# Summing a modulation half-vector on TensorE: as columns with the weight block stationary, instead of as a row and on VectorE

## The chip, the cores and the metric

The program runs on one core of one Trainium2 chip. The metric is device time in microseconds (us) of one execution. The median of three runs of the kernel before is 2114.07 us (2113.8 to 2114.29). The execution that was profiled took 2113.91 us; its span from the first to the last instruction is 2112.2 us.

## The reference

One layer of a streaming encoder on x of 1024 tokens by 1024 features, in float32: a SwiGLU block, a mixer of two attention branches, and a second SwiGLU block. Each of the three sub-layers is modulated by vectors that come from the conditioning vector c:

```python
cond = jax.nn.silu(c)
mod = (cond @ ada_w[l] + ada_b[l]).reshape(B, N_SUBLAYERS, 3, D_MODEL)
h = modulate(x, norm_g[l, 0], mod[:, 0, 0], mod[:, 0, 1])      # shift, scale
x = x + 0.5 * mod[:, 0, 2][:, None, :] * swiglu(h, ffn1_w1[l], ffn1_w3[l], ffn1_w2[l])
```

`modulate` is `rms_norm(x, g) * (1 + scale) + shift`. `ada_w` has 1024 rows and 9 x 1024 columns: column group 0 gives the first shift, group 1 the first scale. The first product of the layer needs h, and so the first shift, the first scale and the root mean square of each token of x.

## The kernel before, in words

x lies transposed: tile `x[i][j]` has 128 features as partitions and 512 of the tokens (half j). The big products are made in float32 from three fast passes each (`mm3`: high part times high, high times low, low times high, where a value is split into a rounded part made by ScalarE and the rest made by VectorE). Such a pass is one MATMUL of 128x512; the tiles `wh`, `wl` are the parts of a weight, and `h` is a part of the modulated x.

All instructions between two calls of `flush` are recorded first and then put in order by a planner (`Plan`). It has a table of prices for each operation (`length`, L359), counts due times back from TensorE's work (`deadlines`), and lets each engine, SyncE's DMA queue among them, take the task that can start first, by due time (`place`). Numbers in `FOUND` (L197) fix, for each flush, the planner's settings and a list of seeds; each seed shifts the due times of a random run of tasks by some us (`moved`). For a flush that `FOUND` does not name, the planner tries the settings in `PLANS` and keeps the best by its own reckoning. There are six flushes: 1 is the opening with the whole first SwiGLU block, 2 the end of that block, 3 and 4 the projections and the index scores, 5 the two attentions, 6 the output products and the second SwiGLU block. An order once chosen is fixed in the program: each engine works its list off in that order and waits where an input is missing.

The opening loads the first token half of x (eight tiles of 256 KB) and the blocks `mraw` of `ada_w`: for a half-vector of 512 columns, eight blocks (kc = 0 to 7) of 128 rows by 512 columns. The class `ModHalf` (L1584) turns the eight blocks into four columns of 128 values in a TensorE bank `b`, and `mod_done` (L1672) adds `ada_b` to them (VectorE, tile `mod`); for the scale it also makes `A`. Two half-vectors are needed for the first product, and before the change they take different ways:

- the scale, `mod[1, 0]`: VectorE multiplies each block by its column of the condition and adds it up in `macc` (`add`, eight instructions); then `columns` (L1609) sums `macc` over its partitions by four matmuls, with a 128x128 block of `macc` stationary and the column `ones_col` moving.
- the shift, `mod[0, 0]`: `row` (L1623) makes eight matmuls with a column of the condition stationary (128x1) and the block moving (512 columns), which gives the sum as a row; ScalarE copies it (`mrow`); `columns_of_row` (L1616) turns it into columns by four matmuls.

These matmuls are plain float32. The list counts one call for each of them; the trace shows two records for each call (four calls on `nacc` are eight records), each with its own LDWEIGHTS, the load of the stationary operand.

Beside that, squares of x (ScalarE, `nsq`) are added on VectorE (`nacc`), summed by four matmuls (`norm_rms`, L676), made into `nr` by twelve small VectorE instructions (`norm_root`), and spread over the partitions by four matmuls with `ident` moving (`norm_spread`, L694). Then `block` (L1716) makes, for four feature tiles, `x <- x * A * spread` (VectorE, `scale`) and the two parts of h (`pair`: ScalarE adds the shift `mod` and rounds, VectorE makes the rest). The weights `wr` of the first products are loaded behind the `mraw` blocks. Four matmuls on zeros (`zr`) that set up banks stand at the very start. The second token half and the modulation half-vectors `mod[1, 1]`, `mod[0, 1]` follow while products run.

Of the kernel before, what the change touches and what calls it, by code (L numbers as in the profile page):

```python
# [16 lines left out]
AF = mybir.ActivationFunctionType  # L17
# [45 lines left out]
class View:  # L63


    def __init__(self, tile, ops):
        self.tile, self.ops = tile, ops
# [117 lines left out]
def real(v):  # L185
# [9 lines left out]
         (10, 0.15, 0, 2, 300, 15, 3), (30, 0.02, 0, 6, 400, 1e9, 2), (30, 0.0, 0, 4, 600, 20, 1), (10, 0.15, 2, 4, 400, 20, 3)]  # L195
VERBOSE = False
FOUND = {  # L197
# [5 lines left out]
}  # L203


# [35 lines left out]
class Plan:  # L241
# [6 lines left out]
    def __init__(self, tc):  # L248
        self.tc, self.on, self.tasks, self.behind = tc, False, [], 0
        self.free = {e: 0.0 for e in self.ENGINES}  # L250
        self.wire, self.done, self.flushes = 0.0, {}, 0
        self.kept, self.wanted, self.spans = {}, [], []
        self.port = {"vector": 0.0, "gpsimd": 0.0}
        for e in self.ENGINES:
            setattr(self, e, PlanEngine(self, e))
# [88 lines left out]
    def close(self):  # L344

        self.on = False
        for x in self.kept.values():
            if x.slot is not None:
                self.slots(x).append((x.end, x.slot))
        self.kept = {}  # L350
# [8 lines left out]
    def length(self, t, e):  # L359

        n = t.n
        if t.dma:
            return 0.06 if e == "sync" else ISSUE, 0.0
        if e == "tensor":
            if t.took:
                return t.took, 0.23
            if t.turn:
                d = TURN[0]
            elif t.exact:
                d = max(0.04, 0.0133 + n / 2400.0) + (0.004 if t.dear and n == 512 else 0.0)  # L370
            elif t.op == "transpose":
                d = n / 1174.0
            else:
                d = max(0.224, 0.009 + n / 595.0)
            return d, 0.23
        more = "accum_out" in t.kw
        if e == "scalar":
            ap = sum(isinstance(t.kw.get(x), View) for x in ("bias", "scale"))
            return (0.055 if t.near else 0.1) + n / 1200.0 + (0.12 if more else 0.0) + (0.06 if ap else 0.0) + (0.13 if t.calls[0][1][0].tile.kw.get("name") == "yt" else 0.0), 0.14
        if e == "gpsimd":  # L380
            if t.op in ("tensor_scalar", "memset"):
                return 0.24 + n / 1230.0, 0.105
            return 0.06 + n / 440.0, 0.105
        if t.op == "tensor_tensor_scan":
            d = 0.15 + n / 480.0
        elif t.op == "tensor_tensor_reduce":
            d = 0.08 + n / 960.0
        elif t.op == "scalar_tensor_tensor" or more:
            d = 0.13 + n / 960.0
        elif t.op == "tensor_scalar" and t.port:  # L390
            d = 0.065 + n / 1920.0
        else:
            d = 0.068 + n / 960.0
        return max(0.09 if t.op == "reciprocal" else 0.075, d), 0.16
# [281 lines left out]
def norm_rms(k, acc, tmp, ptile):  # L676

    nc = k.nc
    ps = ptile()
    for b in range(4):  # L680
        nc.tensor.matmul(ps[:, b:b + 1], acc[:, b * 128:b * 128 + 128], k.ones_col, start=True, stop=True)
    return norm_root(k, ps[:, 0:4], tmp)


def norm_root(k, t, tmp):

    v = tmp.tile([128, 4], F32, tag="nv", name="nv", bufs=1)
    k.nc.vector.tensor_scalar(v, t, 1.0 / D, EPS, op0=ALU.mult, op1=ALU.add)
    r = tmp.tile([128, 4], F32, tag="nr", name="nr", bufs=1)
    rsqrt(k, r, v, tmp, "na", 1)  # L690
    return r
# [892 lines left out]
class ModHalf:  # L1584
# [28 lines left out]
            self.k.nc.tensor.matmul(t[:, b:b + 1], self.acc[:, b * 128:b * 128 + 128], self.k.ones_col, start=True, stop=True)  # L1613
        mod_done(self.k, self.i, t, 4 * self.h, 4)

    def columns_of_row(self, row):  # L1616

        t = self.bank()
        for b in range(4):
            self.k.nc.tensor.matmul(t[:, b:b + 1], row[0:1, b * 128:b * 128 + 128], self.k.ones_col[0:1, :], start=True, stop=True)  # L1620
        mod_done(self.k, self.i, t, 4 * self.h, 4)

    def row(self):  # L1623

        k, nc = self.k, self.k.nc
        t = self.bank()
        for kc in range(8):
            nc.tensor.matmul(t[0:1, :], k.cond[:, kc:kc + 1], self.raws[kc], start=kc == 0, stop=kc == 7)
        r = self.tile("mrow")
        nc.scalar.activation(r[0:1, :], t[0:1, :], AF.Copy)  # L1630
        return r

    def steps(self, d_row):

# [37 lines left out]
def mod_done(k, i, t, b0, n):  # L1672
    nc = k.nc
    m = k.mod[:, i * 8 + b0:i * 8 + b0 + n]
    nc.vector.tensor_add(m, t[:, 0:n], k.ada_b[:, i * 8 + b0:i * 8 + b0 + n])
    s, j = i // 3, i % 3
    c8 = slice(s * 8 + b0, s * 8 + b0 + n)
    if j == 1:
        nc.vector.scalar_tensor_tensor(k.A[:, c8], m, 1.0, k.ng[:, c8], op0=ALU.add, op1=ALU.mult)
    elif j == 2:  # L1680
        nc.vector.tensor_scalar(k.G[:, c8], m, 0.5, None, op0=ALU.mult)
# [540 lines left out]
def layer(tc, xT, c, pos, ada_w, ada_b, ng, inv, w13a, w2a, w_a, w_f, w_q, w_g, fb, fg, dg, wbr, wout, w13b, w2b, out):  # L2222
    with ExitStack() as es:
        k = K()
# [59 lines left out]
        with ExitStack() as ph:  # L2284
# [21 lines left out]
            mod = {(i, h): ModHalf(k, i, h, bank) for h in range(2) for i in range(2)}  # L2306
# [61 lines left out]
                mod[0, 0].load(n + 1)  # L2368
            for i in range(4):
                pairs[i].load1("c", (0,))  # L2370
            rms[0] = norm_rms(k, sq.acc, rp, bank)
            mod[1, 0].add(8)
            ops.rb[0] = norm_spread(k, rms[0], bank)
            row = mod[0, 0].row()
            mod[1, 0].columns()
            mod[0, 0].columns_of_row(row)
            for c in range(4):
                ops.block(c)
            for i in range(4):
# [314 lines left out]
```

## Time and profile before

| | |
|---|---|
| median of three runs | 2114.07 us (2113.8 to 2114.29) |
| the profiled execution | 2113.91 us, span 2112.2 us |
| TensorE busy | 2090.3 us, 99% of the span |
| VectorE busy | 1593.7 us, 75% |
| ScalarE busy | 1126.3 us, 53% |
| GpSimd busy | 356.6 us, 17% |
| first product (`b<-h,wh`) starts | 26.79 us |
| attentions (flush 5) | about 999 to 1295.6 us |

In a row of the timeline stand the start, the length, the engine, the line, the operation, the tile written and the tiles read, the shape and the count of instructions merged into the row; in square brackets the idle time of the engine just before and what ended it. PE is TensorE's matmul, PEld its weight load, DVE VectorE, ACT ScalarE, POOL GpSimd, SPq the issue of DMAs by SyncE. Almost all instructions carry L261, the planner's one issuing line, so they are told apart by their tiles. In a table by stretches of time stand the length of the stretch, the busy time and count of records for each engine, the TensorE clock granted (1.00 is full), the DMA share and the DMA rate.

### The profile page before, as it was taken

What the parts mean: (1) busy time and instruction counts of PE and PEld (TensorE: products, weight loads), DVE (VectorE), ACT (ScalarE), POOL (GpSimd) and SP (SyncE); (2) the same over time, 40 slices, a digit from 0 to 9 for tenths busy, and PEclk for the clock granted to TensorE, in tenths of its full rate; (3) what the DMA queues carried; (4) which work ended last, traced back from release to release, by engine and by line L of the source; (5) the groups of instructions that cost most, each with busy time, mean ns of one, the idle gap of its engine ahead of it and who ended that gap; (6) DMA issues with size and microseconds to landing.
All of it is one profiled execution on the core that took longest, in us unless ns stands there. A gap on an engine that the chain in (4) does not pass through costs nothing.

```text
span 2112.2 us, 31881 instructions
## 1 busy us (share of the span) xinstructions
PE 2090.3 (99%) x10548; PEld 1747.4 (83%) x10548; DVE 1593.7 (75%) x3118; ACT 1126.3 (53%) x2088; POOL 356.6 (17%) x595
## 2 busy tenths in 40 slices
PE   7999999999999999999999999999999999999999
PEld 5888888878888999998888777878888888888887
DVE  7988887869977388775799887697975765558754
ACT  5645444446556285876887775234633333334443
POOL 0013332312101100001545441001011011000000
PEclk9999999999999999999999999999999999999999
DMA  9358887899842325457876766595143434166611
GB/s 356 110 160 292 277 285 258 275 393 387 283 137 98 99 91 196 178 185 255 296 264 232 251 234 245 172 333 192 45 135 124 161 102 138 65 241 253 224 63 43
DMA packets 207959, 429.21 MB, mean 203 GB/s; under 512 B 33192, under 2 KB 51624, under 8 KB 207792
## 3 DMA queue, kind: packets, MB, share of 16 engines
q1 hardware_dynamic: 175392, 321.49, 45.0%
q0 software_dynamic: 32400, 105.67, 13.2%
q8 instruction: 83, 1.36, 0.3%
q14 instruction: 84, 0.69, 0.1%
HBM read 279.48 MB, written 109.83 MB: 184 GB/s over the span
## 4 chain that ended last, share of the span: by engine, by line
PE 92%; DMA 4%; DVE 3%; ACT 1%; issue 1%; SPq 0%; DVEq 0%; ACTq 0%
PE b L261 39%; PE y L261 27%; PE pj L261 13%; PE py L261 7%; PE p L261 4%; PE pt L261 3%; DMA a<-in_w2a 1%; DMA mraw<-in_ada_w 1%; DVE wl L261 0%; DVE h L261 0%; DMA nat<-d_qkv 0%; DMA wr<-in_w13a 0%; DMA wr<-in_wout 0%; DMA pre<-in_w_g 0%; DVE z L261 0%
## 5 line engine op out<-in xcount | busy, mean ns | idle before, releaser
L261 PE MATMUL b<-h,wh 128*128 128x512 f32 x1552 | 483.0, 391 | 2.7 <-ACT h L261 2.6
L261 ACT ACTIVATE wh<-wr 128x512 fp32r<-128x512 f32 x312 | 195.5, 630 | 368.6 <-PE b L261 157.4
L261 PE MATMUL y<-h,wh 128*128 128x512 f32 x1168 | 361.0, 389 | 0.0
L261 PEld LDWEIGHTS b<-h,wh 128*128 128x128 f32 x1552 | 292.1, 189 | 65.4 <-ACT h L261 2.7
L261 DVE TENSOR_TENSOR wl<-wr,wh 128x512 fp32r<-128x512 f32 x312 | 213.0, 687 | 148.6 <-ACT wh L261 148.3
L261 PE MATMUL b<-h,wl 128*128 128x512 f32 x776 | 303.1, 391 | 0.0
L261 PEld LDWEIGHTS y<-h,wh 128*128 128x128 f32 x1168 | 219.1, 188 | 46.1 <-ACT y L261 0.3
L261 PE MATMUL y<-h,wl 128*128 128x512 f32 x584 | 227.2, 389 | 0.0
L261 PE MATMUL pj<-wh,h 128*128 128x384 f32 (+1 forms) x768 | 175.5, 319 | 0.0
L261 PEld LDWEIGHTS b<-h,wl 128*128 128x128 f32 x776 | 146.2, 188 | 30.7
L261 POOL DMA_DIRECT2D d_g<-z x154 | 83.6, 544 | 502.0 <-DVE z L261 485.9
L261 DVE TENSOR_TENSOR wl<-a,wh 128x512 fp32r<-128x512 f32 x132 | 90.6, 687 | 63.6 <-ACT wh L261 61.6
L261 ACT ACTIVATE wh<-g 128x512 fp32r<-128x512 f32 x154 | 96.0, 624 | 78.2 <-PE b L261 49.1
L261 PE MATMUL b<-wl,wh 128*128 128x512 f32 x352 | 136.7, 389 | 0.6 <-DVE wl L261 0.6
L261 ACT ACTIVATE wh<-a 128x512 fp32r<-128x512 f32 x132 | 82.4, 624 | 102.2 <-PE b L261 55.5
L261 PE MATMUL b<-wh 128*128 128x512 f32 x352 | 136.8, 389 | 0.0
L261 PE MATMUL b<-wh,wl 128*128 128x512 f32 x352 | 136.5, 389 | 0.0
L261 PEld LDWEIGHTS pj<-wh,h 128*128 128x128 f32 x768 | 130.2, 189 | 0.8
L261 DVE TENSOR_TENSOR wl<-g,wh 128x512 fp32r<-128x512 f32 x154 | 105.5, 685 | 30.6 <-ACT wh L261 30.6
L261 PEld LDWEIGHTS y<-h,wl 128*128 128x128 f32 x584 | 109.6, 188 | 22.8
L261 PE MATMUL pj<-wl,h 128*128 128x384 f32 (+1 forms) x384 | 113.9, 318 | 0.0
L261 POOL TENSOR_SCALAR pr<-pr,mn 128x896 f32<-128x896 f32 (+7 forms) x128 | 95.2, 756 | 99.8 <-DVE mn L261 56.7
(389 smaller groups left out, 4423.9 us busy)
## 6 DMA issues: line engine op xcount, KB each, us to landing
d_g<-z POOLq DMA_DIRECT2D x154, 256.0 KB, 4.1
g<-d_g SPq DMA_DIRECT2D x154, 256.0 KB, 5.4
mraw<-in_ada_w SPq DMA_DIRECT2D x144, 256.0 KB, 5.4
wr<-in_w13a SPq DMA_DIRECT2D x112, 256.0 KB, 5.2
wr<-in_w13b SPq DMA_DIRECT2D x88, 256.0 KB, 5.1
pc<-pr SPq DMA_DIRECT2D x32, 448.0 KB, 4.4
a<-in_w2a SPq DMA_DIRECT2D x44, 256.0 KB, 6.0
a<-in_w2b SPq DMA_DIRECT2D x44, 256.0 KB, 5.8
```

The costliest lines, as they stand in the source:

```text
L261: getattr(getattr(self.tc.nc, engine), op)(*map(real, a), **{n: real(v) for n, v in kw.items()})
```

## The change

Both half-vectors are now summed by TensorE as columns: for each block and each of its four 128-column parts, one matmul with the 128x128 part stationary and the condition's column (128x1) moving, added up over the eight blocks in the bank. That is 32 calls for a half-vector. The row, its copy, the multiply-adds on VectorE for `mod[1, 0]` and the two small column steps go. The planner's price for a plain float32 matmul becomes lower, its DMA wire starts at 2.4 us, and `FOUND` has new numbers for flush 1 (the opening and the first SwiGLU block) and 5 (the attentions), and an entry for flush 6. The second pair of half-vectors, `mod[1, 1]` and `mod[0, 1]`, stays with `add` and `columns`.

```diff
 FOUND = {
-    1: [(15, 0.0, 0, 2, 900, 20, 3, (501840642, 424298720, 406308056, 19208102, 20202281, 567510933, 399119877, 340876925, 596080701, 1061006555, 18977631, 44916212, 987110367))],
+    1: [(30, 0.0, 0, 4, 600, 20, 1, (217657238, 746267204, 832982268, 106995451, 932333295, 340635646, 173352262, 1061918129, 1066580032, 290986574, 140048833, 716643755, 244607314, 608412914, 249622135, 344545291, 38705008, 729981289, 21257487, 753340328))],
...
+    6: [(3, 0.0, 0, 2, 300, 40, 2, ())],
 }
...
-        self.wire, self.done, self.flushes = 0.0, {}, 0
+        self.wire, self.done, self.flushes = 2.4, {}, 0
...
-                d = max(0.224, 0.009 + n / 595.0)
+                d = max(0.107, 0.05 + n / 1350.0)
...
-    def columns_of_row(self, row):
-
-        t = self.bank()
-        for b in range(4):
-            self.k.nc.tensor.matmul(t[:, b:b + 1], row[0:1, b * 128:b * 128 + 128], self.k.ones_col[0:1, :], start=True, stop=True)
-        mod_done(self.k, self.i, t, 4 * self.h, 4)
-
-    def row(self):
-
-        k, nc = self.k, self.k.nc
-        t = self.bank()
-        for kc in range(8):
-            nc.tensor.matmul(t[0:1, :], k.cond[:, kc:kc + 1], self.raws[kc], start=kc == 0, stop=kc == 7)
-        r = self.tile("mrow")
-        nc.scalar.activation(r[0:1, :], t[0:1, :], AF.Copy)
-        return r
+    def open(self):
+        self.t = self.bank()
+
+    def sums(self, kc):
+
+        k, t = self.k, self.t
+        for b in range(4):
+            first = kc == 0 and b == 0
+            out = t.rearrange("p (h t) -> p h t", h=2)[:, 0, 0:1] if first else t[:, b:b + 1]
+            k.nc.tensor.matmul(out, self.raws[kc][:, b * 128:b * 128 + 128], k.cond[:, kc:kc + 1], start=first, stop=kc == 7,
+                               skip_group_check=True)
+
+    def close(self):
+        mod_done(self.k, self.i, self.t, 4 * self.h, 4)
...
+            for i in (1, 0):
+                mod[i, 0].open()
+            for n in range(4):
+                for i in (1, 0):
+                    mod[i, 0].sums(n)
             rms[0] = norm_rms(k, sq.acc, rp, bank)
-            mod[1, 0].add(8)
             ops.rb[0] = norm_spread(k, rms[0], bank)
-            row = mod[0, 0].row()
-            mod[1, 0].columns()
-            mod[0, 0].columns_of_row(row)
+            for n in range(4, 8):
+                for i in (1, 0):
+                    mod[i, 0].sums(n)
+            for i in (1, 0):
+                mod[i, 0].close()
```

The instructions stand like this on TensorE from the start of the program to the first products, before the change:

```order
L261 MATMUL y<-zr 128x512 x4
L261 MATMUL b<-mraw,cond 1x512 x3
L261 MATMUL b<-ones_col,nacc 128x1 x4
L261 MATMUL b<-mraw,cond 1x512 x5
L261 MATMUL b<-ident,nr 128x128 x4
L261 MATMUL b<-ones_col,mrow 128x1 x2
L261 MATMUL b<-ones_col,macc 128x1 x4
L261 MATMUL b<-ones_col,mrow 128x1 x2
L261 MATMUL b<-h,wh 128x512 x4
```

And on TensorE at the same place after the change (`b<-cond,mraw` are the sums):

```order
L262 MATMUL y<-zr 128x512 x4
L262 MATMUL b<-cond,mraw 128x1 x12
L262 MATMUL b<-ones_col,nacc 128x1 x2
L262 MATMUL b<-cond,mraw 128x1 x4
L262 MATMUL b<-ones_col,nacc 128x1 x2
L262 MATMUL b<-cond,mraw 128x1 x13
L262 MATMUL b<-ident,nr 128x128 x4
L262 MATMUL b<-cond,mraw 128x1 x35
L262 MATMUL b<-h,wh 128x512 x3
```

Between the zeros and the first product stood 8 matmuls with 512 columns moving, 4 with 128 and 12 with one; now there are 68 with one column moving and 4 with 128. The last 20 of the sums are all for the shift; those for the scale are done before them.

On VectorE, the last instructions ahead of the first products, before the change (`x<-x,A,b` is the scaling of a feature tile, `h` the low part, `wl` the low part of a weight):

```order
L261 SCALAR_TENSOR_TENSOR macc<-mraw,cond,macc 128x512 x2
L261 TENSOR_TENSOR wl<-wr,wh 128x512 x2
L261 TENSOR_TENSOR mod<-b,ada_b 128x4 x2
L261 SCALAR_TENSOR_TENSOR A<-mod,ng 128x4
L261 TENSOR_TENSOR wl<-wr,wh 128x512
L261 SCALAR_TENSOR_TENSOR x<-x,A,b 128x512 x3
L261 SCALAR_TENSOR_TENSOR h<-x,mod,h 128x512 x2
```

And on VectorE at the same place after the change:

```order
L262 TENSOR_TENSOR mod<-b,ada_b 128x4
L262 SCALAR_TENSOR_TENSOR A<-mod,ng 128x4
L262 SCALAR_TENSOR_TENSOR x<-x,A,b 128x512 x4
L262 TENSOR_TENSOR mod<-b,ada_b 128x4
L262 TENSOR_TENSOR wl<-wr,wh 128x512
L262 SCALAR_TENSOR_TENSOR h<-x,mod,h 128x512
L262 TENSOR_TENSOR wl<-wr,wh 128x512
L262 SCALAR_TENSOR_TENSOR h<-x,mod,h 128x512 x2
```

The scale is added first, all four feature tiles are scaled, and only then comes the shift; the low parts of the weights have moved behind the shift.

On SyncE's DMA queue, from the start, before the change:

```order
L261 DMA cond<-in_c 128x8
L261 DMA x<-in_xT 128x512 x6
L261 DMA mraw<-in_ada_w 128x512
L261 DMA x<-in_xT 128x512
L261 DMA mraw<-in_ada_w 128x512
L261 DMA x<-in_xT 128x512
L261 DMA mraw<-in_ada_w 128x512 x14
L261 DMA wr<-in_w13a 128x512 x2
```

And on the same queue after the change:

```order
L262 DMA cond<-in_c 128x8
L262 DMA x<-in_xT 128x512 x7
L262 DMA mraw<-in_ada_w 128x512
L262 DMA x<-in_xT 128x512
L262 DMA mraw<-in_ada_w 128x512 x5
L262 DMA ada_b<-in_ada_b 128x72
L262 DMA ng<-in_ng 128x24
L262 DMA mraw<-in_ada_w 128x512 x10
L262 DMA wr<-in_w13a 128x512 x6
```

The first block of `ada_w` stands one place later, behind a seventh tile of x, and the two small loads `ada_b` and `ng` have come forward between the blocks. In the attentions TensorE has the same 2,172 matmuls in another order; the orders of flushes 3 and 4 on TensorE are the same.

2 rows, old and new, of the table FOUND are left out of this document.

## The prediction

> **What bounds the kernel now.** I read the page's head first, then TensorE's waits, then the opening in the timeline, then the granted clock in stretches. From the profile's page:
>
> ```profile
> span 2112.2 us, 31881 instructions
> PE 2090.3 (99%) x10548; PEld 1747.4 (83%) x10548; DVE 1593.7 (75%) x3118; ACT 1126.3 (53%) x2088; POOL 356.6 (17%) x595
> ```
>
> TensorE (PE) is idle for 2112.2 - 2090.3 = 21.9 us. Its waits, longest first:
>
> ```profile
> PE b L261 <- DMA mraw<-in_ada_w: 7.2, 3, 6.1
> PE b L261 <- ACT h L261: 2.6, 1, 2.6
> PE b L261 <- ACT wh L261: 1.7, 1, 1.7
> ```
>
> The first two lie in the opening. Here is PE's timeline from the start to the first products, and a later place with the same column matmuls:
>
> ```profile
> 1.38 2.07 PE L261 MATMUL y<-zr 128*128 128x512 f32 x4 [1.38 <-POOL zr L261]
> 9.60 4.16 PE L261 MATMUL b<-mraw,cond 128*1 128x512 f32 x6 [6.15 <-DMA mraw<-in_ada_w]
> 14.21 1.05 PE L261 MATMUL b<-ones_col,nacc 128*128 128x1 f32 x8 [0.45 <-DVE nacc L261]
> 15.20 1.88 PE L261 MATMUL b<-mraw,cond 128*1 128x512 f32 x4
> ...
> 23.60 0.60 PE L261 MATMUL b<-ones_col,mrow 1*128 1x1 f32 x4
> 26.79 2.08 PE L261 MATMUL b<-h,wh 128*128 128x512 f32 x4 [2.59 <-ACT h L261]
> 28.66 0.63 PE L261 MATMUL b<-h,wl 128*128 128x512 f32 x1
> ...
> 51.56 1.84 PE L261 MATMUL b<-ones_col,macc 128*128 128x1 f32 x16
> 53.26 0.72 PE L261 MATMUL b<-h,wh 128*128 128x512 f32 x2
> ```
>
> From 26.79 us on PE hardly stops, so whatever moves the first product moves the end by as much. Four first products take 28.66 - 26.79 = 1.87 us, 0.47 us each. The reason is the clock (columns: PE busy, PEld, DVE, ACT, POOL, granted clock, DMA):
>
> ```profile
> 9.09:12.51 3.42, 2.91 (x4) 0.40 (x5) 3.11 (x5) 1.33 (x3) 0.00 (x0) 1.00 1.04 370
> ...
> 22.75:26.16 3.41, 1.45 (x12) 1.35 (x12) 3.17 (x8) 3.06 (x6) 0.00 (x0) 1.00 1.05 386
> 26.16:29.57 3.41, 2.78 (x7) 2.20 (x8) 3.41 (x6) 2.26 (x4) 0.00 (x0) 0.50 1.05 383
> 29.57:32.99 3.42, 3.42 (x10) 2.65 (x9) 3.04 (x6) 0.27 (x1) 0.00 (x0) 0.50 1.05 388
> 32.99:36.40 3.41, 3.41 (x17) 2.82 (x16) 1.61 (x3) 2.24 (x5) 0.00 (x0) 1.00 1.05 387
> 1292.51:1295.92 3.41, 1.69 (x8) 1.10 (x7) 1.54 (x3) 2.60 (x5) 1.34 (x3) 1.00 0.76 260
> ```
>
> The clock falls to half at 26.16 and is back at 32.99, two stretches of 3.41 us. In the one before the fall PE was busy 1.45 us, with single-column matmuls alone. At 1292.51 it was busy 1.69 us, hardly more, with 512- and 256-column matmuls, and the clock stayed. So a single-column matmul seems to count little as work for the clock, a moving operand of 512 columns fully: eight of the latter, from 9.60, stand before the full clock of the opening.
>
> **What one sum costs.** A call is two records. At full clock, 8 calls took 53.26 - 51.56 = 1.70 us, 0.21 us each; 4 calls on `nacc` with their start took 15.20 - 14.21 = 0.99 us, 0.25 each. I take 0.22. At half clock no single-column call stands in the trace; its weight load does (minimum, median, maximum in ns of the matmuls on zeros at the start, of `nacc`, and of one-column loads up to 12.5 us):
>
> ```profile
> L261 PEld LDWEIGHTS y<-zr x4: 288/329/338, 1.4 to 2.4; 128*128 128x128 f32 x4
> L261 PEld LDWEIGHTS b<-ones_col,nacc x8: 186/192/193, 14.2 to 15.0; 128*128 128x128 f32 x8
> L261 PEld LDWEIGHTS b<-mraw,cond x5: 79/80/128, 9.6 to 12.4; 128*1 128x1 f32 x5
> ```
>
> Less the 80 ns that a one-column load takes, 128 columns take 186 - 80 = 106 ns at full clock, which is what a record costs in a run (1.70 / 16 = 0.106), and 288 - 80 = 208 ns at the start, where the four matmuls on zeros run as slowly as the first four products (2.07 and 2.08 us). A run of single-column calls is then bound by its loads, at 2 x 0.21 = 0.42 to 0.43 us a call; I take 0.425.
>
> The Trainium skill, "TensorE: Matmul & The Clock Gate", section "LDWEIGHTS (loading the stationary operand)", gives columns / 1.2 ns, 107 ns for 128, without the clock. The trace agrees at full clock (106) and differs at half (208); the measurement decides. By that rule the sums would keep 0.22 us a call.
>
> **The change part by part.** *Start.* The first sum needs the first `mraw` tile, whose issue moves one place back:
>
> ```profile
> 4.08 0.43 SPq L261 DMA_DIRECT2D mraw<-in_ada_w  x1
> 4.56 0.43 SPq L261 DMA_DIRECT2D x<-in_xT  x1
> ...
> 6.61 9.49 SPq L261 DMA_DIRECT2D mraw<-in_ada_w  x14
> ```
>
> That is 4.56 - 4.08 = 0.48 us, so PE starts at 9.60 + 0.48 = 10.08 instead of 9.60. Later blocks come every 9.49 / 14 = 0.68 us, and their four calls take 4 x 0.22 = 0.88 us even at full clock: PE, not the loads, sets the pace, and hides `ada_b` and `ng`, now issued between them.
>
> *PE's work* from there to the first product is 64 sums, 4 calls on `nacc` and 4 on `ident`, 72 calls, each with two loads of 128 columns. At half clock 72 x 0.425 = 30.6 us; at full 72 x 0.22 = 15.8. Nothing in this run brings the full clock if single columns do not count: the four `ident` calls fill half a stretch at most, and 2.78 us of products in a stretch (26.16) did not suffice. I take half: last sum at 10.08 + 30.6 = 40.7.
>
> *Behind the last sum*, today's rows on VectorE and ScalarE:
>
> ```profile
> 24.24 0.16 DVE L261 TENSOR_TENSOR mod<-b,ada_b 128x4 f32<-128x4 f32 x1 [0.19 <-PE b L261]
> 24.32 0.16 DVE L261 SCALAR_TENSOR_TENSOR A<-mod,ng 128x4 f32<-128x4 f32 x1
> ...
> 25.04 2.06 DVE L261 SCALAR_TENSOR_TENSOR x<-x,A,b 128x512 f32<-128x512 f32 x3
> ```
> ```profile
> 26.03 1.93 ACT L261 ACTIVATE h<-x,mod 128x512 fp32r<-128x512 f32 x3
> ```
>
> The last record outlasts its slot by about 0.6 - 4 x 0.11 = 0.15 (row at 23.60), then 0.04 to the addition of the shift, 0.16 for it, about 0.25 to ScalarE, 1.93 / 3 = 0.64 for h, and 26.79 - 26.67 = 0.12 to PE: 1.4 us. `A` and the four scalings (0.16 + 0.16 + 4 x 2.06 / 3 = 3.1 us) run beside the last 20 sums, all for the shift (8.5 us, or 4.4 at full clock); without that cover they would cost up to 3.1. First product at 40.7 + 1.4 = 42.1, 15.3 later than now.
>
> *Queued behind that wait:* on VectorE `wl` and the low parts of h, on ScalarE `wh`; PE waits for them in the first products. At half clock PE takes 0.43 us for each product against about 0.7 us for each such tile, which serves several products: 0 us, at most 1.
>
> *Clock in the first products.* Two products at half clock, and two at full:
>
> ```profile
> 29.09 1.05 PE L261 MATMUL b<-h,wh 128*128 128x512 f32 x2
> 29.94 0.63 PE L261 MATMUL b<-h,wl 128*128 128x512 f32 x1
> ...
> 34.10 0.62 PE L261 MATMUL b<-h,wh 128*128 128x512 f32 x2
> 34.56 0.39 PE L261 MATMUL b<-h,wl 128*128 128x512 f32 x1
> ```
>
> From start to start that is 0.85 / 2 = 0.43 and 0.46 / 2 = 0.23 us. Today's 26.79 to 32.99 at half costs 6.2 x (1 - 0.23 / 0.43) = 2.9 us. After the change it costs between 1.6 and 3.2 (3.4 to 6.8 us at half), by where in a stretch the products begin: -0.5, bounds -1.3 and +0.3.
>
> *Taken away:* the row (PE, inside the run above), 8 VectorE instructions of 0.5 to 0.75 us and a ScalarE copy. They make `nr` ready earlier, but `ident` stands behind 29 sums: 0.
>
> *The other orders.* After the opening PE waits 26.8 to 421.8 for 0.1 us, and in the attentions for 4.4:
>
> ```profile
> 26.80:421.80 395.00, 394.90 (x1743) 326.18 (x1744) 335.33 (x585) 204.79 (x364) 95.70 (x178) 0.99 0.73 246
> ...
> 999.00:1295.60 296.60, 292.24 (x2170) 233.26 (x2169) 252.22 (x553) 226.73 (x500) 141.29 (x190) 1.00 0.74 260
> ```
>
> A new order of the same matmuls can win part of these 4.4 us, 1.7 of them at the seam, and lose as much: 0, bounds -2 and +2.
>
> **Sum:** 2113.91 + 15.3 - 0.5 = 2128.7 for an execution like the profiled one, which is 0.16 under the median of 2114.07; on that median 2128.9 us, with its own range 2126.5 to 2131.5.
>
> **Rivals.**
>
> *Not slower: the sums count as work.* Place: the stretches from 9.09 to 15.92. If a record with one moving column counts like its load, the full clock comes at 12.5 or 15.9; 5.7 or 13.7 calls are slow, the rest (66.3 or 58.3) take 14.6 or 12.8 us, so the sums end at 27.1 or 28.7 and the first product starts at 28.5 or 30.1, 1.7 to 3.3 later. With PE then idle for only 1.4 us the clock holds, which saves 2.9: -1.2 to +0.4, about 2113.7. For it: a one-column stationary operand did count (9.09). Against: 1.45 us of such records did not hold the clock at 22.75, where 1.69 us of others did. It decides if more than about 8 in 10 of a stretch count. The Trainium skill, same page, "Part 1: The HAM clock gate", has any 3.4 us of sustained matmuls release the clock, which is this rival; its "Part 4: PE-mode transpose" says that transposes do not count in the same way. No run here shows either for a run of sums.
>
> *The load does not slow down.* Half clock, but 0.22 a call: 10.08 + 15.8 + 1.4 = 27.3, +0.5, and the clock loss as today: 2114.6. Against it stands 208 against 106 ns.
>
> *The planner's new price is right:* 0.107 us a call. Then blocks of 0.43 us hide behind loads of 0.68, the last of which lands about 10.08 + 16 x 0.68 = 21.0, and the first product starts at 21.0 + 0.4 + 1.4 = 22.8: -4.0, or -6.9 with the clock held; 2108 to 2110. Against: 8 calls took 1.70 us.
>
> **How the numbers follow.** Forecast 0.67, sums count 0.19, load not slowed 0.06, planner's price 0.05, and 0.03 for something else. The range 2111 to 2131.5 takes in the forecast's own range, the second and the third case. About 0.2% (4.2 us) is what a measurement of this kernel can tell from no change. Faster 0.07 (the price, and tails of the second case), same 0.24, slower 0.69.
>
> **What would show it.** Right: the granted clock is half until after the first products begin, the loads of the sums take about 0.29 to 0.33 us and the first product starts near 42; VectorE's four scalings lie beside the last sums. Wrong: the clock is full before 16 us, the sums run at 0.11 us a record, or PE waits for `mraw` between the sums.

## The result, and the profile after

The changed kernel takes 2137.24 us (median of five executions, 2135.34 to 2138.56), the kernel before 2114.07 us: 1.0109 times as long, 95% interval 1.0094 to 1.0124. It is slower by some 23 us; forecast were 15. The profiled execution took 2137.26 us, against 2113.91. From the head of the page of after:

```profile
span 2135.4 us, 31983 instructions
PE 2112.6 (99%) x10644; PEld 1778.5 (83%) x10644; DVE 1590.3 (74%) x3110; ACT 1124.4 (53%) x2087; POOL 358.7 (17%) x595
```

TensorE is busy for 2112.6 us, 22.3 more than before, and idle for 22.8, hardly more than the 21.9 of before: almost all of the added time counts as TensorE's work. In the timeline of PE, the opening:

```profile
10.57 5.25 PE L262 MATMUL b<-cond,mraw 128*128 128x1 f32 x24 [7.12 <-DMA mraw<-in_ada_w]
15.69 0.99 PE L262 MATMUL b<-ones_col,nacc 128*128 128x1 f32 x4
16.54 1.85 PE L262 MATMUL b<-cond,mraw 128*128 128x1 f32 x8
18.25 0.99 PE L262 MATMUL b<-ones_col,nacc 128*128 128x1 f32 x4
19.10 5.69 PE L262 MATMUL b<-cond,mraw 128*128 128x1 f32 x26
24.65 2.05 PE L262 MATMUL b<-ident,nr 128*128 128x128 f32 x8
26.50 14.93 PE L262 MATMUL b<-cond,mraw 128*128 128x1 f32 x70
42.44 1.74 PE L262 MATMUL b<-h,wh 128*128 128x512 f32 x3 [1.01 <-ACT h L262]
...
47.81 0.63 PE L262 MATMUL b<-h,wl 128*128 128x512 f32 x1
48.24 0.69 PE L262 MATMUL b<-h,wh 128*128 128x512 f32 x2
48.77 0.40 PE L262 MATMUL b<-h,wl 128*128 128x512 f32 x1
```

From 10.57 to 26.50 + 14.93 = 41.43 PE works without a wait: 30.86 us for 72 calls, 0.429 us each. The first product starts at 42.44, 15.65 later than before. The products stay slow (0.63 us a record) until about 48.3 and are fast (0.40) from then on. The loads of the sums (minimum, median and maximum in ns):

```profile
L262 PEld LDWEIGHTS b<-cond,mraw x128: 288/333/338, 10.5 to 41.0; 128*128 128x128 f32 x128
```

They have the length that loads had at half clock (333 ns in the median, against 186 to 193 at full). The clock column itself can't show it here: the trace's record of the clock begins only at 48.37 us, with a change to full, and stretches ahead of the first entry are printed as 1.00. That 333 ns means half clock is read off a run further down, where the clock is on record while such sums run (`after_wide`). On VectorE, behind the sums for the scale and behind the last sum:

```profile
32.93 0.16 DVE L262 TENSOR_TENSOR mod<-b,ada_b 128x4 f32<-128x4 f32 x1 [11.31 <-PE b L262]
...
33.33 2.72 DVE L262 SCALAR_TENSOR_TENSOR x<-x,A,b 128x512 f32<-128x512 f32 x4
41.47 0.16 DVE L262 TENSOR_TENSOR mod<-b,ada_b 128x4 f32<-128x4 f32 x1 [5.42 <-PE b L262]
```

The four scalings lie beside the last sums. PE's waits, longest first (us in total, times, longest):

```profile
PE b L262 <- DMA mraw<-in_ada_w: 7.1, 1, 7.1
PE b L262 <- ACT wh L262: 3.2, 2, 1.7
PE pj L262 <- DMA wh<-d_wf03h: 2.0, 1, 2.0
PE pj L262 <- DMA wl<-d_wf03l: 1.8, 1, 1.8
```

Before, `wh` was waited for once; the two waits of the projections (`pj`) are new. Beside them stands the clock (columns as in the prediction):

```profile
608.16:611.57 3.41, 1.86 (x7) 1.05 (x6) 3.20 (x6) 3.41 (x7) 2.15 (x4) 1.00 1.06 394
611.57:614.98 3.41, 3.41 (x9) 2.67 (x8) 1.55 (x3) 0.93 (x3) 0.00 (x0) 0.50 0.57 201
...
731.04:734.45 3.41, 0.44 (x1) 0.19 (x1) 0.00 (x0) 0.00 (x0) 0.00 (x0) 1.00 0.92 339
734.45:737.86 3.41, 2.54 (x8) 2.54 (x9) 0.00 (x0) 0.49 (x1) 0.00 (x0) 0.50 1.04 386
737.86:741.27 3.41, 3.41 (x13) 3.41 (x12) 0.00 (x0) 0.00 (x0) 0.00 (x0) 0.50 0.78 296
```

Each wait drew half clock after it: one stretch at 611.57, two at 734.45. The prediction's rate, 1 - 0.23 / 0.43 = 0.47 lost of each us at half clock, makes that 1.6 and 3.2 us. This is a cost that stands in no list of waits.

The starts of the same work in the two timelines say where the 23 us came from:

| start of | before | after | later by |
|---|---|---|---|
| first product | 26.79 | 42.44 | 15.65 |
| first `b<-h,wa` (late in flush 2) | 669.15 | 688.33 | 19.18 |
| first projection `pj` | 708.54 | 727.72 | 19.18 |
| first transpose `pt` behind the projections | 731.60 | 757.95 | 26.35 |
| first attention product `py` | 998.87 | 1025.45 | 26.58 |
| first `b<-yh,wh` (flush 6) | 1295.60 | 1320.91 | 25.31 |
| end of PE | 2108.03 | 2131.30 | 23.27 |

So the opening cost 15.65, the first block 3.5, the projections 7.2 and the step to the attentions 0.2, while attentions and last flush gave back 1.3 and 2.0.

Why the projections wait shows on SyncE's queue, in the two loads for the fourth projection weight. Before:

```profile
685.66 0.32 SPq L261 DMA_DIRECT2D wh<-d_wf03h  x1
689.19 0.32 SPq L261 DMA_DIRECT2D wl<-d_wf03l  x1
```

After:

```profile
729.27 0.32 SPq L262 DMA_DIRECT2D wh<-d_wf03h  x1
729.70 0.39 SPq L262 DMA_DIRECT2D wl<-d_wf03l  x1
```

With everything 19 us later they come 44 and 41 us later, when PE already works on the projections. The orders give no reason, the allocation does. The buffers of this weight and the next share their memory with slots 0 to 7 of a pool of small tiles; `wh` of the fourth weight lies on slots 0 and 1, its `wl` on 2 and 3. The eight `nat` tiles of flush 2 take whichever slots of that pool the planner holds free soonest. Before, these were slots between 15 and 49; after, they were 20, 44, 43, 29, 0, 14, 9 and 4. So the fifth `nat` tile lies in slot 0, and the load of `wh` must wait until it is stored. The chain of work that ended last has that store just ahead of the load:

```profile
726.98 2.23 DMA d_na<-nat
```

It lands at 729.21, and the load goes out at 729.27. (The expectation for `after_nat` below speaks of the last `nat` tile; it is the fifth.) PE's order there is the same in both kernels, and so the views of the orders did not show it. With the sums alone (the first run below) slot 0 holds the fourth `nat` tile, which is stored earlier: there the load goes out at 704.02, in time.

### The profile page after: what moved, and what is told of

It reads as the page before. It is cut to its first block, busy times and chain, and to the rows that moved or that the text cites. A ratio compares the mean times of both kernels' runs of the same rounds, so it can differ in the third digit from the quotient of the medians.

```text
span 2135.4 us, 31983 instructions
## 1 busy us (share of the span) xinstructions
PE 2112.6 (99%) x10644; PEld 1778.5 (83%) x10644; DVE 1590.3 (74%) x3110; ACT 1124.4 (53%) x2087; POOL 358.7 (17%) x595
## 4 chain that ended last, share of the span: by engine, by line
PE 84%; issue 11%; POOL 2%; DMA 1%; ACT 1%; DVE 0%; SPq 0%; POOLq 0%; ACTq 0%
PE b L262 34%; PE y L262 24%; PE pj L262 13%; PE py L262 7%; PE p L262 4%; PE pt L262 2%; POOL d_x L262 0%; DMA d_wg12l<-pre 0%; DMA mraw<-in_ada_w 0%; DMA wl<-d_wf03l 0%; DMA wl<-d_wg13l 0%; SPq L262 0%; POOL d_g L262 0%; DMA yr<-d_y 0%; ACT pr L262 0%
## 5 line engine op out<-in xcount | busy, mean ns | idle before, releaser
L262 DVE TENSOR_TENSOR ptl<-pt,pth 128x512 fp32r<-128x512 f32 (+2 forms) x160 | 98.7, 631 | 16.9 <-ACT pth L262 15.4
```

Of the source, the lines that this page charges most:

```text
L262: getattr(getattr(self.tc.nc, engine), op)(*map(real, a), **{n: real(v) for n, v in kw.items()})
```

## The experiments

**The theories.** *A:* the excess of about 7.5 us over opening and clock comes from the new numbers for the planner: they fix other orders and slots for the work up to the projections, with waits of their own. *B:* it comes from the late opening itself, whatever the planner, since all of the later work was fitted to a start near 27 us. And for the sums: that their 0.43 us is the clock's doing (*theory*), or that such a matmul into one bank is slow in itself (*rival*).

**Sums alone: the changed kernel with the planner's numbers of before.**

```diff
-FOUND = {1: [(30, ...)], ..., 5: [...], 6: [...]}
+FOUND = {1: [(15, ...)], ..., 5: [...]}
-        self.wire, self.done, self.flushes = 2.4, {}, 0
+        self.wire, self.done, self.flushes = 0.0, {}, 0
-                d = max(0.107, 0.05 + n / 1350.0)
+                d = max(0.224, 0.009 + n / 595.0)
```

> The new sums alone: both half-vectors summed as columns, but the planner's price, its wire and all of its numbers as before the change. Theory (the sums cost what half the clock makes of 72 calls, and the rest of the loss comes from the new numbers, not from the late start): the first product starts at 40 to 44 us, 13 to 17 us later than the 26.79 us before, and the time is 2126 to 2132 us, without the waits that the changed kernel has near 608 and 730 us. Rival (the late start itself puts the later loads out of step): the later waits are there too, in sum about 10 us, and the time is 2135 to 2139 us.

It took 2127.48 us (2126.44 to 2127.63; the kernel before beside it 2113.41): ratio 1.0063, interval 1.0048 to 1.0078. PE's timeline:

```profile
4.27 19.76 PE L261 MATMUL b<-cond,mraw 128*128 128x1 f32 x92 [0.81 <-DMA mraw<-in_ada_w]
...
36.92 2.07 PE L261 MATMUL b<-h,wh 128*128 128x512 f32 x4 [1.59 <-ACT h L261]
```

The first product came earlier than I had expected, at 36.92, since this order loads `mraw` ahead of x and starts the sums at 4.27; 46 calls in 19.76 us are again 0.43 us each. The starts were 10.1 us late at the first product, 10.9 at the first `pj` and 12.2 at the end, the last step being one stretch at half clock at 1307.58. PE has no wait near 608 or 730. An opening that is 10 us late does not by itself bring those waits, which speaks for theory A and against B.

**The new numbers alone: the kernel before, row and `add` kept, with the price, wire and `FOUND` of after.**

```diff
-        self.wire, self.done, self.flushes = 0.0, {}, 0
+        self.wire, self.done, self.flushes = 2.4, {}, 0
-                d = max(0.224, 0.009 + n / 595.0)
+                d = max(0.107, 0.05 + n / 1350.0)
-FOUND = {1: [(15, ...)], ..., 5: [...]}
+FOUND = {1: [(30, ...)], ..., 5: [...], 6: [...]}
```

> The new planner price, wire and numbers alone, with the opening's row and multiply-adds as before the change. Since the seeds move other tasks here, the order of the first block is a third one. Theory (the sums are the greater loss): the first product starts at 26 to 29 us and the time is within 2110 to 2120 us. Rival (the lower price alone makes a bad opening or a bad first block): over 2122 us.

2121.30 us (2119.35 to 2123.97), ratio 1.0036 (1.0023 to 1.0049): a little above what was expected. Its first product starts at 29.75 (+3.0). PE's waits, the longest:

```profile
PE b L262 <- DVE nacc L262: 9.2, 1, 9.2
PE y L262 <- ACT u L262: 3.0, 1, 3.0
...
PE b L262 <- DVE xc L262: 1.6, 2, 1.3
```

The waits of 3.0 (up to 646 us) and 1.3 (up to 582) stand in the first block, where before had none of that length; its start of `pj` is 7.7 late, 3.0 of it from the opening. They are not the same waits as in after, since the seeds meet another list of tasks, and the projections have none here (from the first `pj` to the first `pt` 23.07 us, against 23.06 in before). So the new numbers cost about 8 us without any sum, for the greater part in waits, but after's own waits come only where they meet the sums. The two ratios multiply to 1.0063 x 1.0036 = 1.0099, near the 1.0109 of both together; since the waits are others, that is in part chance.

**After, with the `nat` tiles kept out of slots 0 to 7.** The two lines ahead of flush 2 tell the planner that these slots come free late; PE's order stays as it is.

```diff
+            c0 = id(k.homes["c"][0])
+            nc.done = {s: [(a + 1000.0 * (s[0] == c0 and i < 8), i) for a, i in v] for s, v in nc.done.items()}
```

> The changed kernel, same order on TensorE, but in the second flush the tiles nat are kept out of the memory that the fourth projection weight wf03 is later loaded into. Theory (the load of wf03 waits at 729.2 us for the last nat tile to be stored, since it lies in the same memory; the wait then halves the clock for 6.8 us): the two waits of 2.0 and 1.8 us go, and with them the half clock, which cost 6.8 x 0.47 = 3.2 us: 7.1 us less, about 2130 us. Rival (the load is late because everything is late, or the transfers are full): the waits stay, 2136 to 2138 us.

2129.73 us (2128.74 to 2131.62), ratio 1.0076 (1.0061 to 1.0091), 7.5 us below after; the intervals do not touch. PE's waits, from the second on:

```profile
PE b L262 <- ACT wh L262: 3.0, 2, 1.7
PE y L262 <- POOL zr L262: 1.4, 1, 1.4
PE b L262 <- ACT h L262: 1.0, 1, 1.0
...
PE pj L262 <- DMA wl<-d_wf03l: 0.4, 1, 0.4
```

Of the 3.8 us at the projections 0.4 are left, and there is no half clock there: from the first `pj` to the first `pt` it takes 23.75 us, against 30.23 in after and 23.06 in before. The allocation was the cause of these waits. The opening is 15.15 late here too, so its lateness is not (theory B). The first block's wait near 608 stayed (1.33 us), but in this execution drew no half clock, which makes that block 2.3 us shorter than after's; the last flush lost 1.6 us to a half clock that after did not have. Of the gain, 6.5 us are thus the projections'.

**After, with broad matmuls among the sums.** More matmuls on zeros, whose result nothing uses, are to bring the full clock and hold it: 18 ahead of the sums, two behind each four sums, four ahead of the first product.

```diff
+WIDE = {4: 18, 8: 2, 12: 2, ..., 72: 2, 76: 4}
...
         for s, _, t, e, _ in self.trace:
             for c in t.calls:
                 self.issue(e, *c)
+            n += e == "tensor"
+            for _ in range(WIDE.get(n, 0) if e == "tensor" and self.flushes == 1 else 0):
+                self.issue("tensor", *self.zeros)
+            if n == 1 and e == "tensor" and self.flushes == 1:
+                self.zeros = t.calls[0]
```

> The changed kernel with more of its 128x512 matmuls on zeros, which change no result: 18 before the sums, 2 after each block of four sums, 4 before the first product; all other instructions as they are. Theory (the sums are slow because of the half clock, and single-column calls do not count as work for it): the weight loads of the sums take 0.19 us instead of 0.33, a sum 0.22 us instead of 0.43; 72 x 0.22 + 30 x 0.23 = 22.7 us from 10.6 us on, so the first product starts at 34 to 36 us instead of 42.4 and runs at full clock; 7 us and 2.8 us less, about 2127 us. Rival (the sums are slow in themselves, by the fresh weight load or the adding in one bank): a sum stays at 0.43 us, the zeros come on top, and the time is 2141 to 2145 us. If the later waits depend on the late start, they shrink too and the time is near 2120 us.

2145.85 us (2143.93 to 2147.48), ratio 1.0148 (1.0131 to 1.0165): no remedy. The time is near the one that the rival gave, but not by the rival's cause. PE's timeline:

```profile
10.57 1.02 PE L264 MATMUL b<-cond,mraw 128*128 128x1 f32 x8 [1.67 <-DMA mraw<-in_ada_w]
11.46 0.71 PE L264 MATMUL y<-zr 128*128 128x512 f32 x2
12.01 0.95 PE L264 MATMUL b<-cond,mraw 128*128 128x1 f32 x8
12.82 1.07 PE L264 MATMUL y<-zr 128*128 128x512 f32 x2
13.68 1.70 PE L264 MATMUL b<-cond,mraw 128*128 128x1 f32 x8
15.24 1.20 PE L264 MATMUL y<-zr 128*128 128x512 f32 x2
```

And the clock in the same run:

```profile
6.15:9.56 3.41, 2.75 (x12) 1.88 (x10) 2.00 (x4) 2.35 (x4) 0.00 (x0) 1.00 0.99 353
9.56:12.97 3.41, 2.40 (x19) 2.32 (x20) 2.34 (x4) 1.44 (x3) 0.00 (x0) 1.00 1.05 398
12.97:16.38 3.41, 3.41 (x14) 3.03 (x14) 0.00 (x0) 0.00 (x0) 0.00 (x0) 0.50 1.04 364
```

The zeros brought the full clock at 6.15, but two of them for four sums did not hold it past 12.97; then it stayed half until 57.35. Yet the run settles the question that it was made for. Four sums of the same kind take 0.22 us each up to 12.97 (11.46 - 10.57 = 0.89 for four) and 0.39 just behind it (15.24 - 13.68 = 1.56 for four). Their weight loads, up to 12.9 us and from 13 us on:

```profile
L264 PEld LDWEIGHTS b<-cond,mraw x16: 186/192/192, 10.5 to 12.7; 128*128 128x128 f32 x16
L264 PEld LDWEIGHTS b<-cond,mraw x112: 330/333/338, 13.3 to 51.7; 128*128 128x128 f32 x112
```

The second row lies wholly in stretches with 0.50 on record, and its 333 ns are those of after's sums. The clock makes their cost, not the bank. And with a start 11 us later than after's the waits of the projections are there again (1.8 and 1.2 us), so they do not hang on the exact lateness either.

**Three parts on the kernel before, and all three together.** *One:* eleven matmuls on zeros in PE's gap ahead of the first product, to hold the clock through it (the hook above, with `WIDE = {28: 11}`).

> The kernel before the change with eleven more of its 128x512 matmuls on zeros, behind the last single-column matmul of the opening, where TensorE was idle for 2.6 us; they change no result. Theory (the clock falls when less than about four tenths of a stretch of 3.41 us are spent streaming moving columns; single-column matmuls count as nothing): from 24.07 us on 11 x 0.21 = 2.3 us are streamed, six tenths of the stretch in which the clock fell, so it stays, the first products take 0.23 us instead of 0.43 from the first on, and 2.9 us go: about 2110.5 us. Rival (the clock falls by another rule, or the first products wait for h in its place): no gain, 2113 to 2114 us, with half the clock at 26 to 33 us or waits in the first products.

2113.72 us (2112.30 to 2117.75, eleven executions) beside 2113.33 for before (2111.29 to 2117.94, 33): ratio 1.0002 (0.9994 to 1.0011). No gain that can be measured, where 2.9 us was expected. In the profiled execution (2112.30 us) the clock held and the first `pj` came 3.1 us earlier than in before; 2.0 of it were left at PE's end. The mean granted clock was 1.000 in three of the eleven executions and 0.997 to 0.999 in the others, so the zeros did not hold it every time; and the three took 2112.30, 2112.95 and 2113.72 us, little less than before's median.

*Two:* only the new numbers for the attentions.

```diff
-    5: [... as before ...],
+    5: [... as after ...],
```

> The kernel before the change with the new numbers of the attentions (flush 5) alone. Theory (their order wins what the changed kernel's trace shows there, 1.3 us): 2112 to 2113 us. Rival (it only looked so because of where the clock's stretches fell): 2113.5 to 2114.5 us.

2112.22 us (2111.72 to 2113.42), ratio 0.9992 (0.9983 to 1.0001): in the expected place, not clear of no change. The attentions as one stretch:

```profile
997.84:1293.63 295.79, 292.51 (x2170) 234.48 (x2170) 253.62 (x553) 227.78 (x500) 141.87 (x190) 1.00 0.75 261
```

PE idles 3.3 us in them instead of 4.4.

*Three:* only the new entry for the last flush.

```diff
+    6: [(3, 0.0, 0, 2, 300, 40, 2, ())],
```

> The kernel before the change with the new entry for the last flush (output products and second SwiGLU block) alone. Theory (the changed kernel's last stage is 2.0 us shorter because its settings were not the ones that the planner chose before): 2111.5 to 2112.5 us. Rival (the gain hung on the state that the attentions leave): 2113.5 to 2115 us.

2111.22 us (2109.11 to 2112.99), ratio 0.9990 (0.9981 to 0.9999). The last flush takes 810.38 us on PE, where the starts of before give 812.43.

*All three:*

> The kernel before the change with the eleven matmuls on zeros and the new numbers of flushes 5 and 6, and without the new sums, price, wire and numbers of the first block. Theory (the three gains lie in stages apart and add up): 2.9 + 1.3 + 2.0 = 6.2 us less, about 2107.8 us, faster than both kernels. Rival (one of them gives the other's gain back): 2110 us or more.

2109.17 us (2107.90 to 2111.02), ratio 0.9981 (0.9972 to 0.9990): 4.2 us faster than before and 28 faster than after. The gains of two and three add up, 1.1 + 2.1 = 3.2; what the zeros add is within the spread. So the change held a small gain, and by the medians it lay in the numbers for flushes 5 and 6, not in the sums; that of flush 5 alone is not clear of no change.

## Why the prediction was wrong

Slower was right, and so was the mechanism of the opening, but the size was some 8 us short: 2137.2 lies above the range.

- *Start of the sums:* put at 10.08, measured 10.57.
- *72 calls at 0.425 us, 30.6 us:* measured 30.86. Taking half clock and the load as the limit of a call held.
- *Tail of 1.4 us, scalings covered:* measured 42.44 - 41.43 = 1.01, with the scalings done at 36.05. The first product was put 15.3 us later and came 15.65 later.
- *Half clock in the first products, -0.5:* half clock lasted from 42.44 to 48.37, where the clock's record begins, 5.9 us against 6.2 before: -0.1, within its bounds.
- *Queued behind that wait, 0 us:* no wait for `wh`, `wl` or a low part of h came in the first products.
- *"The other orders": 0, bounds -2 and +2. This step failed.* It measured 3.5 + 0.1 + 7.2 + 0.2 - 1.3 - 2.0 = +7.7 (the first block's 3.5 holds the -0.1 of the clock, which is a term of its own). With it the sum closes: 2113.91 + 15.65 - 0.1 + 7.7 = 2137.2, against 2137.26 measured.

The step failed in three ways. It asked only what a new order could win or lose of waits that before had (0.1 us up to 421.8, 4.4 in the attentions), and left 421.8 to 999 out, where the greater part of the loss came. A kernel in which PE hardly waits has nearly nothing to win there and everything to lose, so the bounds should have lain on the slow side. It then took the same order of TensorE's work in flushes 3 and 4 for the same cost, though new numbers for flush 1 pass on through what the planner believes to be free: the slots that flush 2 picks. The run with the `nat` tiles moved shows that 6.5 us were this. And it priced a wait at its own length. The 3.8 us at the projections cost 7.2, because two stretches at half clock follow.

What made the first block 3.5 us longer is less settled. PE waits for `wh` at 609.88, and ScalarE is late with it. From ScalarE's timeline of after:

```profile
607.25 0.63 ACT L262 ACTIVATE pre<-pre 128x512 fp32r<-128x512 f32 x1 [4.21 <-issue]
608.15 0.63 ACT L262 ACTIVATE pre<-pre 128x512 fp32r<-128x512 f32 x1 [0.28 <-DMA d_wg14l<-pre]
608.69 0.61 ACT L262 ACTIVATE wh<-g 128x512 fp32r<-128x512 f32 x1
```

It stands before two roundings of a later weight (`pre`), the second of which waits for a store, while `wh` is queued behind them. That the wait needs the new numbers is shown (with the sums and the old numbers it is absent); that these two roundings make it is read from the queue and wasn't tried. 1.45 us of wait and 1.6 of half clock make 3.0 of the 3.5.

*The rivals.* That the sums count as work for the clock fell: 31 us of them did not raise it. The sign that the prediction named for that, the granted clock, has no entry in the record for the opening; the length of the loads stands in for it. "Part 1: The HAM clock gate" in "TensorE: Matmul & The Clock Gate" of the Trainium skill, by which some 3.4 us of sustained matmuls release it, does not agree with this trace for matmuls of one column. That the load does not slow down, as a formula without the clock would have it ("LDWEIGHTS (loading the stationary operand)" in "TensorE: Matmul & The Clock Gate" of the Trainium skill), fell as well: 333 ns in the median at half clock, 192 at full (`after_wide`). The planner's price of 0.107 us fell with them; a call took four times that. The chances told the sign; the range, bounded by the same 2 us, was too narrow on the slow side.

## What to carry to other kernels

Where TensorE is busy for 99% of the span, the price of a new order is counted from what it can lose. After any change of a planner's numbers, compare which buffers and slots the tiles get, as well as the order, and look for loads that must wait for another tile's memory. A matmul with one column moving costs its weight load and earns no clock, so 64 of them ahead of the first product take what the clock allows, not what the planner was told. A wait of 1.5 to 4 us on a full TensorE may cost twice its length.

## What the runs showed of the hardware

**The clock follows the columns that stream, not the time that PE is busy.** Here are two stretches of the last kernel (all three parts together), with PE busy for all of the first:

```profile
21.67:25.08 3.41, 3.41 (x26) 3.16 (x25) 2.69 (x7) 2.83 (x6) 0.00 (x0) 1.00 1.05 365
25.08:28.49 3.41, 3.41 (x10) 2.66 (x9) 3.41 (x6) 3.04 (x5) 0.00 (x0) 0.50 1.01 365
```

And a stretch of after, in which and behind which the clock is full:

```profile
1318.13:1321.54 3.41, 1.69 (x9) 1.06 (x7) 1.84 (x3) 2.90 (x6) 1.20 (x2) 1.00 0.76 259
```

The fully busy one, mostly single columns, lost the clock; the half-empty one, 256 and 512 columns at a time, kept it. I counted for each stretch of 3.41 us the time in which moving columns stream (0.21 us for a fast pass of 512 at full clock, twice that for each record of a plain float32 matmul, and twice all of it at half clock). In these traces the border lies at a share of about 0.38: the clock fell after less (0.33 in the first row above, 0.34 at 608.16, 0.18 at 9.56 among the broad matmuls) and held after more (0.39 in the last row). It rose after 0.82 or more and stayed half at up to 0.77. One stretch does not fit: with the new numbers alone the clock held behind 0.37, in the stretch from 2112.46. This reckoning is fitted to the traces, not tried by itself.

**The stretches run by themselves.** Their borders lie otherwise against the program's start in each execution (12.51 in before, 13.78 with the eleven zeros, 14.84 in the last kernel, which are not whole stretches of 3.41 apart). So the same wait may or may not lose the clock: the wait ahead of flush 6, 1.72 us in all kernels, did so with the sums alone, with the new numbers alone and with the `nat` tiles moved, and not in before. The eleven zeros held the clock in one profiled execution and not in the other. So a gain that depends on the border's place, like the zeros', is easily overrated from one trace. In the 33 executions of before the ten with a mean granted clock of 0.999 have a median of 2112.03 us and the seventeen with 0.998 one of 2113.88, but the six with 0.997 one of 2113.75: the clock is a part of their spread, not all of it.
